# First stage in longer instructions, with places of split weights as three of 8 KB

## The chip, the cores and the metric

The kernel runs on one core of a Trainium2 chip. The metric is the device time in microseconds (us), the median of several runs. The core has five engines that matter here, each with a queue that is worked off in order: TensorE (PE in the profile, its weight loads PEld), VectorE (DVE), ScalarE (ACT), GpSimd (POOL) and SyncE (SP), which issues nearly all loads. Matmuls write to PSUM, eight banks of 2 KB per partition; everything else lies in SBUF, 128 partitions wide.

## The reference

One transformer layer on 256 tokens of width 2048, in fp32. Nine vectors ("ada") of width 2048 come from a condition c, and each of the three parts shifts and scales its input by them. FFN width is 5632.

```python
def _swiglu(h, w_in, w_out):
    gate, up = jnp.split(h @ w_in, 2, axis=-1)
    return (jax.nn.silu(gate) * up) @ w_out

def _layer(x, c, w_ada, b_ada, ffn1_w_in, ffn1_w_out, ...):
    ada = (jax.nn.silu(c) @ w_ada + b_ada)[:, None, :]
    sh1, sc1, g1, sh2, sc2, g2, sh3, sc3, g3 = jnp.split(ada, N_ADA, axis=-1)
    h = _swiglu(_modulate(x, sh1, sc1), ffn1_w_in, ffn1_w_out)
    x = _layernorm(ALPHA * x + 0.5 * (1 + g1) * h, ln1_g, ln1_b)
    h = _token_mixer(_modulate(x, sh2, sc2), w_in, ..., w_out)      # attention and mLSTM
    x = _layernorm(ALPHA * x + (1 + g2) * h, ln2_g, ln2_b)
    h = _swiglu(_modulate(x, sh3, sc3), ffn2_w_in, ffn2_w_out)
    return _layernorm(ALPHA * x + 0.5 * (1 + g3) * h, ln3_g, ln3_b)
```

`_modulate(x, shift, scale)` is `layernorm(x) * (1 + scale) + shift`.

## The kernel before

**Products.** Every large product is made of three matmuls on fp32r parts (`mm3`): a value is split into hi (rounded) and lo (the rest), and hi by hi, hi by lo and lo by hi are added up in PSUM. The activations are split once (`xhi`, `xlo`). The weights are split chunk by chunk as they come in (`load_w`): one load of 1 MB into one of three "raw" places, then per half chunk a cast on ACT (hi, line 145) and a subtraction on DVE (lo = raw - hi, line 146). Six places of 4 KB per partition hold the hi halves and six the lo halves.

**Stage one** is the first FFN's input product for the first 12 of 22 groups of 256 hidden columns, with their up halves. It begins before the ada vectors are known: the 2048 input rows are worked in four groups j of 512, since the group j needs only the quarter of shift and scale that `first_ada(j)` has computed. Per group there are 12 chunks i (even: gate columns, odd: up columns) of 512 rows by 512 columns; each is 48 matmuls 128x256, with starts 0.113 us apart, 5.4 us in all. That gives 48 chunks, here numbered 12 j + i. A chunk's result fills two banks (tiles s), and `first_in` adds it up over j in SBUF: group 0 is copied by ACT (line 738), groups 1 to 3 are added by DVE (line 740), one bank at a time. The parts lie in `hT` (places hT_0 to hT_3) and, for the last chunk of a group, in the unused half of `gate`. In group 3 the finished pair goes through Silu (ACT, line 744) into a small tile `sgs` and a product (DVE, line 745), each per 128x256.

**The ada work beside it.** While group j is multiplied, `first_ada(j+1)` loads 16 rows of 0.5 MB of w_ada (tiles ar), twelve of them by twos in raw places, four in places of their own, and DVE accumulates each into `acc` (lines 158, 160). Four column sums on PE (line 691, tiles cp and cq, one bank each) turn the accumulator into columns; DVE adds the bias (`scsh`, line 693), ACT scales the transposed input by them and splits it (lines 292, 295; xlo is DVE's line 297). In group 3, DVE accumulates for later ada vectors instead (`pump`).

**Then** `ffn_in` computes the other 10 groups of hidden columns (tiles gu_f, weights f1i), the output products follow (o_f), the mixer (fv, mv: loads of 4 x 128 rows by 512 or 520 columns through `cols_form_b`; mo, pr_f), and the second FFN (gu, f2i, f2o).

**Order.** The program is written as generators that are drawn in turn; a scheduler puts each engine's instructions into one fixed queue by their expected readiness, and loads are issued by SP in one queue, each when its place is free. PSUM is two pools for the whole kernel: five banks for results (`mm_tile`) and three for the rest (`aux_tile`); a tile takes the next bank in turn and waits for whoever last read it.

## Time and profile before

| | |
|---|---|
| runs | 1969.59, 1971.78, 1976.58 us; median 1971.78 |
| profiled execution | 1967.35 us, of which the span 1965.6 |
| mean granted TensorE clock | 0.995 |
| busy: PE, DVE, ACT | 1900.2 (97%), 1486.1 (76%), 944.3 (48%) us |
| data moved | 510.91 MB, mean 260 GB/s |
| stage one | from 37.85 to 316.2 us |

Times in the trace are us from the start of the span. A row of the timeline has start, duration, engine, line, operation, result<-inputs, shape and, in brackets, how long the engine had been idle and who released it; "x2" joins two instructions in a row. A row of a group has the count, the busy time, the mean of one in ns and the idle time ahead of it with its releasers. A row of waits has the sum, the count and the longest. Matmul ends are modelled, so what an engine loses is read from the distance of the starts.

### The profile page before, as it was taken

The page shows a single profiled execution, that of the slowest core. Times are in us where ns is not written, and L with a number is a line of the kernel's source. Part 1 is how long each engine was busy: PE and PEld are TensorE (multiplying, and loading weights), DVE is VectorE, ACT ScalarE, POOL GpSimd, SP SyncE. Part 2 cuts the span into 40 slices and gives each one's busy share as a digit, 9 for nine tenths or more (in the row PEclk, how much of TensorE's full clock was granted, in tenths as well). Part 3 has the DMA queues.
Part 4 walks back from the last instruction along what each step waited for, and adds up shares of the span by engine and source line. Part 5 has one row for each costly group of instructions (what it writes and reads, how often), then busy time and mean ns, then how long its engine had stood idle before and what let it go on. Part 6 is the DMA issues. An engine that isn't in the chain of part 4 may idle for free.

```text
span 1965.6 us, 32416 instructions
## 1 busy us (share of the span) xinstructions
PE 1900.2 (97%) x13201; PEld 1736.7 (88%) x13201; DVE 1486.1 (76%) x1827; ACT 944.3 (48%) x1328; POOL 19.6 (1%) x34
## 2 busy tenths in 40 slices
PE   3999999999999999999999999999999999999997
PEld 3999999999988888588999876899999999988886
DVE  7788888777778898678888687778756645555776
ACT  2544354443444554645755543555444444444552
POOL 0000000000000000000000000000000000000000
PEclk9999999999999999999999999999999999999998
DMA  9999878989989785589888784898757855655552
GB/s 335 333 326 315 309 234 294 310 291 303 317 297 310 269 292 199 174 302 298 268 299 287 266 276 147 293 297 296 260 194 254 278 194 187 236 191 192 193 193 86
DMA packets 301822, 510.91 MB, mean 260 GB/s; under 512 B 10819, under 2 KB 158691, under 8 KB 300649
## 3 DMA queue, kind: packets, MB, share of 16 engines
q1 hardware_dynamic: 300808, 505.70, 76.5%
q0 software_dynamic: 864, 3.15, 0.5%
q8 instruction: 103, 1.69, 0.4%
q14 instruction: 47, 0.38, 0.1%
HBM read 506.71 MB, written 2.10 MB: 259 GB/s over the span
## 4 chain that ended last, share of the span: by engine, by line
PE 77%; DMA 9%; DVE 9%; ACT 2%; issue 2%; POOL 0%; SPq 0%; DVEq 0%; ACTq 0%; POOLq 0%
PE o_f L355 8%; PE o_f L357 8%; PE o_f L356 8%; PE gu_f L355 7%; PE gu_f L357 7%; PE gu_f L356 7%; DMA ar<-in_w_ada_dram 5%; PE s L357 3%; PE s L355 3%; PE s L356 3%; DVE acc L160 2%; PE pr_f L356 2%; PE pr_f L355 2%; PE pr_f L357 2%; PE fs L355 1%
## 5 line engine op out<-in xcount | busy, mean ns | idle before, releaser
L160 DVE SCALAR_TENSOR_TENSOR acc<-ar,csil,acc 128x1024 f32<-128x1024 f32 x242 | 307.7, 1272 | 106.7 <-DMA ar<-in_w_ada_dram 105.3
L355 PE MATMUL s<-xhi_f,hi_s 128*128 128x256 f32 x768 | 213.8, 279 | 0.8 <-ACT hi_s L145 0.6
L357 PE MATMUL s<-xhi_f,lo_s 128*128 128x256 f32 x768 | 213.1, 278 | 0.6 <-DVE lo_s L146 0.5
L356 PE MATMUL s<-xlo_f,hi_s 128*128 128x256 f32 x768 | 213.4, 278 | 0.0
L357 PE MATMUL gu_f<-xhi_f,lo_f2i 128*128 128x256 f32 x768 | 212.0, 276 | 0.0
L355 PE MATMUL gu_f<-xhi_f,hi_f2i 128*128 128x256 f32 x768 | 212.0, 276 | 0.0
L356 PE MATMUL gu_f<-xlo_f,hi_f2i 128*128 128x256 f32 x768 | 212.0, 276 | 0.0
L146 DVE TENSOR_TENSOR lo_f2i<-raw_f2i,hi_f2i 128x1024 fp32r<-128x1024 f32 x96 | 116.8, 1223 | 89.5 <-ACT hi_f2i L145 89.5
L355 PE MATMUL gu_f<-xhi_f,hi_f1i 128*128 128x256 f32 x640 | 176.8, 276 | 0.2 <-DVE hT L740 0.2
L357 PE MATMUL gu_f<-xhi_f,lo_f1i 128*128 128x256 f32 x640 | 176.7, 276 | 0.0
L356 PE MATMUL gu_f<-xlo_f,hi_f1i 128*128 128x256 f32 x640 | 176.7, 276 | 0.0
L145 ACT CAST hi_f2i<-raw_f2i 128x1024 fp32r<-128x1024 f32 x96 | 100.4, 1049 | 133.7 <-PE gu_f L356 112.4
L355 PEld LDWEIGHTS s<-xhi_f,hi_s 128*128 128x128 f32 x768 | 145.1, 189 | 1.1 <-ACT hi_s L145 0.7
L357 PEld LDWEIGHTS s<-xhi_f,lo_s 128*128 128x128 f32 x768 | 144.9, 189 | 1.1 <-DVE lo_s L146 1.1
L356 PEld LDWEIGHTS s<-xlo_f,hi_s 128*128 128x128 f32 x768 | 145.2, 189 | 0.3 <-DVE xlo_f L297 0.3
L356 PEld LDWEIGHTS gu_f<-xlo_f,hi_f2i 128*128 128x128 f32 x768 | 144.1, 188 | 0.2
L355 PEld LDWEIGHTS gu_f<-xhi_f,hi_f2i 128*128 128x128 f32 x768 | 144.1, 188 | 0.2
L145 ACT CAST hi_s<-raw_s 128x1024 fp32r<-128x1024 f32 x96 | 97.3, 1050 | 97.5 <-DMA raw_s<-in_ffn_w_in_dram 56.6
L357 PEld LDWEIGHTS gu_f<-xhi_f,lo_f2i 128*128 128x128 f32 x768 | 144.1, 188 | 0.0
L146 DVE TENSOR_TENSOR lo_f2o<-raw_f2o,hi_f2o 128x1024 fp32r<-128x1024 f32 x88 | 107.7, 1224 | 44.9 <-ACT hi_f2o L145 44.8
L355 PE MATMUL o_f<-hi_f2o,hh 128*128 128x512 f32 (+1 forms) x368 | 139.4, 379 | 0.0
L357 PE MATMUL o_f<-hi_f2o,hl 128*128 128x512 f32 (+1 forms) x368 | 138.7, 377 | 0.0
(451 smaller groups left out, 5342.0 us busy)
## 6 DMA issues: line engine op xcount, KB each, us to landing
ar<-in_w_ada_dram SPq DMA_DIRECT2D x288, 512.0 KB, 5.7
raw_s<-in_ffn_w_in_dram SPq DMA_DIRECT2D x48, 1024.0 KB, 6.0
raw_f2i<-in_ffn_w_in_dram SPq DMA_DIRECT2D x48, 1024.0 KB, 5.1
raw_f1o<-in_ffn_w_out_dram SPq DMA_DIRECT2D x44, 1024.0 KB, 6.9
raw_f2o<-in_ffn_w_out_dram SPq DMA_DIRECT2D x44, 1024.0 KB, 5.1
raw_f1i<-in_ffn_w_in_dram SPq DMA_DIRECT2D x40, 1024.0 KB, 7.7
raw_mxo<-in_w_out_dram SPq DMA_DIRECT2D x16, 1024.0 KB, 6.8
raw_fh<-in_ffn_w_in_dram SPq DMA_DIRECT2D x16, 1024.0 KB, 7.5
```

The costliest lines, as they stand in the source:

```text
L145: S.copy(hi, src)
L146: V.tensor_tensor(out=lo, in0=src, in1=hi.bitcast(F32), op=ALU.subtract)
L160: V.scalar_tensor_tensor(out=acc, in0=raw, scalar=csil[:, k:k + 1], in1=acc, op0=ALU.mult, op1=ALU.add)
L355: PE.matmul(o, ah, bh, start=start, stop=False)
L356: PE.matmul(o, ah, bl, start=False, stop=False)
L357: return PE.matmul(o, al, bh, start=False, stop=stop)
```

## The change

Four things are altered.

- The places of split weights are three of 8 KB for hi and three for lo, each for a whole chunk (`part_tiles`). Outside stage one the casts and subtractions stay as they were, half a chunk each, and write into halves of a place.
- In stage one, from its second chunk on, `load_w` is called with `wide`: ACT casts the two halves, and then one subtraction makes the low part of the whole chunk (128x2048).
- A chunk's two result banks are one tile (`mm_pair`); copies, sums, Silu and products work on 128x1024, Silu in its place. The four column sums of a group lie in one such tile (cp). For stage one PSUM is divided into three pairs and two single banks (pools pm1, pa1); these are given back before `ffn_in`, and the pools of five and three are opened there.
- Where `cols_form_b` loads 520 columns, a load has 2 x 128 rows in place of 4 x 128, so there are eight of 0.53 MB per group in place of four.

```diff
     wp.tile([P, 4, 520], F32, tag="raw", bufs=3, name="raw_place")
     gap(wp, 320, "gap_hi")
-    wp.tile([P, 1024], F32R, tag="hi", bufs=6, name="hi_place")
+    wp.tile([P, 2048], F32R, tag="hi", bufs=3, name="hi_place")
...
-    wp.tile([P, 1024], F32R, tag="lo", bufs=6, name="lo_place")
+    wp.tile([P, 2048], F32R, tag="lo", bufs=3, name="lo_place")
...
-    pm = ctx.enter_context(tc.tile_pool(name="pm", bufs=5, space=PSUM))
-    pa = ctx.enter_context(tc.tile_pool(name="pa", bufs=3, space=PSUM))
+    pm = tc.alloc_tile_pool(name="pm1", bufs=3, space=PSUM)
+    pa = tc.alloc_tile_pool(name="pa1", bufs=2, space=PSUM)
...
+    def mm_pair(name):
+        return pm.tile([P, 2, 512], F32, tag="mm2", name=name)
...
+    def part_tiles(nk, w, name):
+        return [wp.tile([P, nk, w], F32R, tag=t, bufs=3, name=f"{t}_{name}") for t in ("hi", "lo")]
+
-    def load_w(src, nk, w, name, place=None):
+    def load_w(src, nk, w, name, place=None, wide=False):
         raw = wp.tile([P, nk, w], F32, tag="raw", bufs=3, name=f"raw_{name}")
         SP.dma_start(raw, src.rearrange("(k p) n -> p k n", p=P))
-        h = nk // 2 if nk * w <= 2048 else nk // 4
-        for q in range(nk // h):
...
-            hi = wp.tile([P, h, w], F32R, tag="hi", bufs=6, name=f"hi_{name}{q}")
-            lo = wp.tile([P, h, w], F32R, tag="lo", bufs=6, name=f"lo_{name}{q}")
-            split(raw[:, q * h:(q + 1) * h, :], hi, lo)
-            for kk in range(h):
-                yield q * h + kk, hi[:, kk, :], lo[:, kk, :]
...
+        hi, lo = part_tiles(nk, w, name)
+        h = nk // 2
+        for q in range(2):
+            ks = slice(q * h, (q + 1) * h)
+            if wide:
+                S.copy(hi[:, ks], raw[:, ks])
+            else:
+                split(raw[:, ks], hi[:, ks], lo[:, ks])
+                for k in range(q * h, (q + 1) * h):
+                    yield k, hi[:, k, :], lo[:, k, :]
+        if wide:
+            V.tensor_tensor(out=lo, in0=raw, in1=hi.bitcast(F32), op=ALU.subtract)
+            for k in range(nk):
+                yield k, hi[:, k, :], lo[:, k, :]
...
-        cps = aux_tile(f"cp{j}"), mm_tile(f"cq{j}")
+        cps = mm_pair(f"cp{j}")
 
         def column(q):
-            cp = cps[q % 2][:, q:q + 2]
+            cp = cps[:, q % 2, q:q + 2]
...
-        for k, hi, lo in load_w(W1[j * 512:(j + 1) * 512, c0:c0 + 512], 4, 512, f"s{j}_{i}"):
+        for k, hi, lo in load_w(W1[j * 512:(j + 1) * 512, c0:c0 + 512], 4, 512, f"s{j}_{i}", wide=i + j > 0):
             yield 4 * j + k, hi, lo
 
     def first_in(j, i, ws):
         gu, q = i % 2, i // 2
-        pss = [mm_tile(f"s{j}_{i}_{b}") for b in range(2)]
+        ps2 = mm_pair(f"s{j}_{i}")
...
-        for b, ps in enumerate(pss):
-            f0 = 2 * NS * gu + 4 * q + 2 * b
-            part = first_part(f0, f0 + 2).rearrange("p f t -> p (f t)")
-            if j == 0:
-                S.copy(part, ps)
-            else:
-                V.tensor_tensor(out=part, in0=part, in1=ps, op=ALU.add)
-            if j == 3 and gu:
-                for f in range(f0, f0 + 2):
-                    sg = sm.tile([P, T], F32, tag="sg", bufs=2, name=f"sgs{f}")
-                    S.activation(sg, hT[:, f - 2 * NS, :], AF.Silu)
-                    V.tensor_tensor(out=hT[:, f - 2 * NS, :], in0=sg, in1=first_part(f, f + 1)[:, 0, :], op=ALU.mult)
+        f0 = 2 * NS * gu + 4 * q
+        part = first_part(f0, f0 + 4).rearrange("p f t -> p (f t)")
+        ps = ps2.rearrange("p b n -> p (b n)")
+        if j == 0:
+            S.copy(part, ps)
+        else:
+            V.tensor_tensor(out=part, in0=part, in1=ps, op=ALU.add)
+        if j == 3 and gu:
+            f1 = f0 - 2 * NS
+            g = hT[:, f1:f1 + 4, :].rearrange("p f t -> p (f t)")
+            S.activation(g, g, AF.Silu)
+            V.tensor_tensor(out=g, in0=g, in1=part, op=ALU.mult)
...
     npool.release()
+    pa.release()
+    pm.release()
+    pm = ctx.enter_context(tc.tile_pool(name="pm", bufs=5, space=PSUM))
+    pa = ctx.enter_context(tc.tile_pool(name="pa", bufs=3, space=PSUM))
     ffn_in(W1, xT, hT, NS, "f1", at(R_IN))
...
-        for u in range(4):
-            for k4, hi, lo in load_w(W[u * 512:(u + 1) * 512, c0 + col:c0 + col + cb[-1]], 4, cb[-1],
+        kn = 4 if cb[-1] <= 512 else 2
+        for u in range(KD // kn):
+            for k_, hi, lo in load_w(W[u * kn * P:(u + 1) * kn * P, c0 + col:c0 + col + cb[-1]], kn, cb[-1],
                                      f"{name}{col}_{u}"):
```

The change also reorders the queues. On DVE at the start of stage one the order before was (lo_s_10 is the first half of chunk 1's low part, ar_1_k are rows of w_ada for group 1):

```order
L146 TENSOR_TENSOR lo_s_10_311<-raw_s_1_308,hi_s_10_310 128x1024
L146 TENSOR_TENSOR lo_s_11_315<-raw_s_1_308,hi_s_11_314 128x1024
L160 SCALAR_TENSOR_TENSOR acc_1_300<-ar_1_1_368,csil,acc_1_300 128x1024 x2
L160 SCALAR_TENSOR_TENSOR acc_1_300<-ar_1_4_435,csil,acc_1_300 128x1024
L146 TENSOR_TENSOR lo_s_20_378<-raw_s_2_375,hi_s_20_377 128x1024
L160 SCALAR_TENSOR_TENSOR acc_1_300<-ar_1_5_437,csil,acc_1_300 128x1024
L146 TENSOR_TENSOR lo_s_21_382<-raw_s_2_375,hi_s_21_381 128x1024
```

and is now:

```order
L363 TENSOR_TENSOR lo_s_1_305<-raw_s_1_302,hi_s_1_304 128x2048
L163 SCALAR_TENSOR_TENSOR acc_1_295<-ar_1_1_358,csil,acc_1_295 128x1024 x2
L163 SCALAR_TENSOR_TENSOR acc_1_295<-ar_1_4_420,csil,acc_1_295 128x1024
L163 SCALAR_TENSOR_TENSOR acc_1_295<-ar_1_5_422,csil,acc_1_295 128x1024
L363 TENSOR_TENSOR lo_s_2_367<-raw_s_2_364,hi_s_2_366 128x2048
```

Both accumulations that stood around the first half of chunk 2's low part now stand ahead of the whole of it. On DVE at the end of stage one the order before was (f1i are weights of `ffn_in`; s_10 and s_11 are the last two chunks of group 3, and the sum into gate is that of the very last):

```order
L740 TENSOR_TENSOR hT_3_111<-hT_3_111,s_10_0_3440 128x512
L740 TENSOR_TENSOR hT_3_111<-hT_3_111,s_10_1_3441 128x512
L146 TENSOR_TENSOR lo_f1i_0_10_3652<-raw_f1i_0_1_3649,hi_f1i_0_10_3651 128x1024
L146 TENSOR_TENSOR lo_f1i_0_11_3680<-raw_f1i_0_1_3649,hi_f1i_0_11_3679 128x1024
L160 SCALAR_TENSOR_TENSOR acc_0_3007<-ar_0_12_3707,csil,acc_0_3007 128x1024
L146 TENSOR_TENSOR lo_f1i_1_00_3713<-raw_f1i_1_0_3710,hi_f1i_1_00_3712 128x1024
L740 TENSOR_TENSOR gate<-gate,s_11_0_3508 128x512
L740 TENSOR_TENSOR gate<-gate,s_11_1_3509 128x512
```

and is now:

```order
L754 TENSOR_TENSOR hT_3_111<-hT_3_111,s_10_3157 128x1024
L149 TENSOR_TENSOR lo_f1i_0_1_3355<-raw_f1i_0_1_3352,hi_f1i_0_1_3354 128x1024 x2
L163 SCALAR_TENSOR_TENSOR acc_0_2784<-ar_0_13_3467,csil,acc_0_2784 128x1024
L163 SCALAR_TENSOR_TENSOR acc_0_2784<-ar_0_14_3526,csil,acc_0_2784 128x1024
L754 TENSOR_TENSOR gate<-gate,s_11_3220 128x1024
L149 TENSOR_TENSOR lo_f1i_1_0_3414<-raw_f1i_1_0_3411,hi_f1i_1_0_3413 128x1024
```

Rows 13 and 14 of the later ada vector stand ahead of the last sum now, where before row 12 was the last there; one low half stands behind it. On PE the first matmul of `ffn_in` is, in both, the one behind the last of s_11. Now:

```order
L368 MATMUL s_11_3220<-xhi_f_120,hi_s_11_3223 128x256
L369 MATMUL s_11_3220<-xlo_f_121,hi_s_11_3223 128x256
L370 MATMUL s_11_3220<-xhi_f_120,lo_s_11_3224 128x256
L368 MATMUL gu_f_0_3291<-xhi_f_120,hi_f1i_0_0_3295 128x256 [waits DVE_49,Activation_49]
L369 MATMUL gu_f_0_3291<-xlo_f_121,hi_f1i_0_0_3295 128x256
L370 MATMUL gu_f_0_3291<-xhi_f_120,lo_f1i_0_0_3296 128x256
```

The value of DVE's counter that this matmul waits for is reached by the sum into gate of s_11 (line 754), since its bank lies in the pair that this chunk held. Before, the same wait was for the second sum of s_9 (line 740), and the other gu_f of the pair waited for the first of s_10.

## The prediction

> **What bounds the kernel now.** I read the page's shares and slices first, then the waits and groups of stage one (38 to 317 us), then each stop of TensorE there.

> ```profile
> PE 1900.2 (97%) x13201; PEld 1736.7 (88%) x13201; DVE 1486.1 (76%) x1827; ACT 944.3 (48%) x1328; POOL 19.6 (1%) x34
> PE   3999999999999999999999999999999999999997
> PEclk9999999999999999999999999999999999999998
> ```

> TensorE is the bound in every slice but the first and the last. Faster VectorE work pays only where TensorE stops. It stops in stage one at these places, and 316.10 is the stage's last matmul:

> ```profile
> 55.28 0.51 PE L357 MATMUL s<-xhi_f,lo_s 128*128 128x256 f32 x2 [0.52 <-DVE lo_s L146]
> 104.59 0.61 PE L691 MATMUL cp<-trir,acc 128*128 128x1 f32 x4 [0.51 <-DVE scsh L693]
> 177.11 0.61 PE L691 MATMUL cp<-trir,gate 128*128 128x1 f32 x4 [2.60 <-DVE scsh L693]
> 310.95 0.38 PE L355 MATMUL s<-xhi_f,hi_s 128*128 128x256 f32 x1 [0.21 <-DVE hT L740]
> 316.10 0.28 PE L357 MATMUL s<-xhi_f,lo_s 128*128 128x256 f32 x1
> 316.21 0.28 PE L355 MATMUL gu_f<-xhi_f,hi_f1i 128*128 128x256 f32 x1
> 316.96 0.38 PE L355 MATMUL gu_f<-xhi_f,hi_f1i 128*128 128x256 f32 x1 [0.24 <-DVE hT L740]
> ```

> Starts are 0.11 us apart when nothing waits, so by starts these cost 0.68, 0.67, 2.76, 0.37 and 0.40: 4.9 us, 0.25% of the time. That is all that can be won there. A gain over 0.3% (5.9 us, about what a measurement of this kernel can tell from no change) has no place to come from; a loss has no such limit.

> **The change part by part.** *Longer VectorE instructions.* Their rows:

> ```profile
> L146 DVE TENSOR_TENSOR lo_s<-raw_s,hi_s 128x1024 fp32r<-128x1024 f32 x96 | 114.1, 1219 | 28.0 <-ACT hi_s L145 28.0
> L740 DVE TENSOR_TENSOR hT<-hT,s 128x512 f32<-128x512 f32 x66 | 42.1, 679 | 0.0
> L745 DVE TENSOR_TENSOR hT<-sgs,hT 128x256 f32<-128x256 f32 x20 | 7.5, 417 | 0.0
> 89.40 2.36 DVE L146 TENSOR_TENSOR lo_s<-raw_s,hi_s 128x1024 fp32r<-128x1024 f32 x2 [1.15 <-ACT hi_s L145]
> 91.90 0.28 PE L357 MATMUL s<-xhi_f,lo_s 128*128 128x256 f32 x1
> ```

> Two lows take 2.36, so the second starts 1.14 after the first, though one is busy for 1.22. Two sums of 128x512 take 1.27 (rows below), 0.60 apart. Per 512 elements that is 0.54, and 0.06 fixed. Joined are 47 pairs of lows, 36 of sums and 18 (24 products to 6): 101 x 0.06 = 6 us of VectorE in the stage's 279. Under a busy TensorE that is worth nothing by itself.

> [...]

> *Lows of a whole chunk* come later for their first user. Before, the first half is ready after one cast and one subtraction; now after two casts (2.00) and one subtraction of 2.36-0.06 = 2.3: about 2.06 later. The second half, and the raw place with it, is 0.9 later (4.35 from landing, before 3.45). It counts where lows are late already, behind loads in j=0:

> ```profile
> 50.59 1.05 ACT L145 CAST hi_s<-raw_s 128x1024 fp32r<-128x1024 f32 x1 [3.26 <-DMA raw_s<-in_ffn_w_in_dram]
> 52.65 1.06 ACT L145 CAST hi_s<-raw_s 128x1024 fp32r<-128x1024 f32 x1
> 53.10 0.49 PE L357 MATMUL s<-xhi_f,lo_s 128*128 128x256 f32 x2
> 54.01 1.22 DVE L146 TENSOR_TENSOR lo_s<-raw_s,hi_s 128x1024 fp32r<-128x1024 f32 x1
> ACT hi_s L145 <- DMA raw_s<-in_ffn_w_in_dram: 56.6, 20, 7.2
> ```

> Chunk 2 (its casts start at 50.59): both casts in a row end at 52.6, the low at 54.9, or 56.2 if the accumulation that now stands ahead of it is late; I take 55.2. The first use stood at 53.10: 2.1 lost, less the 0.68 of 55.28 that goes: **+1.5** (0 to +2.5). Chunk 1 stops about 1.1, inside these 2.1. Chunk 9's first low was done at 90.63 for a use at 91.90, 1.3 to spare where 2.06 is needed; TensorE, later by 1.5, then has 0.7 left. But the three raw places serve 12 chunks and 6 pairs of ada rows a group, so a place turns in two chunks, and each turn is up to 0.9 longer, in j=0 up to the tenth chunk four turns, 3.6. I take **+1.3** (0 to +4.4). After that casts wait more for TensorE than for loads, and lows have over 4 us to spare.

> *Column sums.* At 104.59 the accumulator's column sum waited for its bank; the order now has other work there: **-0.7**. At 177 the wait is an ada load's:

> ```profile
> 174.50 1.28 DVE L160 SCALAR_TENSOR_TENSOR acc<-ar,csil,acc 128x1024 f32<-128x1024 f32 x1 [3.40 <-DMA ar<-in_w_ada_dram]
> 176.90 0.15 DVE L693 TENSOR_TENSOR scsh<-cp,bcol 128x2 f32<-128x2 f32 x1
> ```

> TensorE comes 2.1 later (1.5+1.3-0.7). A load that lands at a fixed time gives that back; one that waits for a place doesn't. Half: -1.1. One tile now holds all four column sums, so each waits for the addition of the last (0.15 and a turn between engines), and the last quarter's xlo stands behind a sum of 1.2: +0.5, and +0.2 at the next group. **-0.4** (-2.8 to +3).

> *The end of the stage.* Stage one now has its own pools: three pairs of banks and two. They are given back before ffn_in, whose first gu_f takes the first bank, in the pair of the very last sum (gate, chunk s_11 of j=3). So that matmul waits for VectorE's last sum; before, it waited for the sum of s_9, two chunks earlier. VectorE's rows there:

> ```profile
> 260.27 1.22 DVE L146 TENSOR_TENSOR lo_s<-raw_s,hi_s 128x1024 fp32r<-128x1024 f32 x1 [1.88 <-ACT hi_s L145]
> L160 DVE SCALAR_TENSOR_TENSOR acc<-ar,csil,acc 128x1024 f32<-128x1024 f32 x12 | 15.4, 1279 | 3.6 <-DMA ar<-in_w_ada_dram 3.6
> 316.23 1.27 DVE L740 TENSOR_TENSOR hT<-hT,s 128x512 f32<-128x512 f32 x2
> 317.42 2.35 DVE L146 TENSOR_TENSOR lo_f1i<-raw_f1i,hi_f1i 128x1024 fp32r<-128x1024 f32 x2
> 319.69 1.27 DVE L160 SCALAR_TENSOR_TENSOR acc<-ar,csil,acc 128x1024 f32<-128x1024 f32 x1
> 322.03 1.27 DVE L740 TENSOR_TENSOR gate<-gate,s 128x512 f32<-128x512 f32 x2
> ```

> Its last sum ended at 323.30, 7 us after TensorE's last matmul, and nobody cared. From 260.27, where it was level with TensorE (it waited for a cast), that is 63.0, of which 3.8 were waits (3.6 for ada loads). Now: 59.2 of work, less 34 joints x 0.06 = 2.0, less one low half that moved behind the sum (1.14), plus two accumulations that moved ahead of it (2.4): 58.5. It ends at 318.8 without a wait, at 322.5 with 3.7 as before. TensorE would be there at 315.8 (316.21 without the 0.37 of 310.95, which three pairs remove): a stop of 3.0 or 6.7; less the 0.77 of before: +2.3 or +5.9. I take **+5.9**, as the ada loads stand in the same traffic. If VectorE were level at the last chunk, two lows, two accumulations and a sum (5.9) against a chunk's 5.4 leave 0.5, a last sum 1.2 and a handover 0.1: +1.0, the low end. One more late load of 3.4 (the longest here, at 174.50): +9.3, the high end.

> *The clock behind it.* Such a stop can cost a stretch at half clock:

> ```profile
> 843.97 0.39 PE L355 MATMUL b_fv<-hi_fv,xhi_mx 128*128 128x264 f32 x1 [1.95 <-ACT og L1144]
> 842.00:845.40 3.40, 1.45 (x10) 1.27 (x10) 2.69 (x3) 3.39 (x10) 0.00 (x0) 0.99 0.71 238
> 845.40:848.80 3.40, 3.40 (x18) 3.40 (x17) 2.00 (x6) 1.69 (x4) 0.00 (x0) 0.50 0.81 258
> 174.50:181.00 6.50, 3.90 (x35) 3.89 (x35) 6.50 (x13) 4.56 (x10) 0.73 (x1) 1.00 0.51 165
> ```

> After 1.95 us idle 3.4 us ran at 0.50, so 1.7 were lost; after 2.60 idle (177.11) the clock stayed at 1.00. A stop of 6.7 is far longer than both: **+1.7** (0, or 3.4 with one at chunk 2). [...]

> *The rest.* Places of 8 KB are returned a chunk at a time, loads of 520 columns are halved:

> ```profile
> ACT hi_f2i L145 <- PE gu_f L356: 112.4, 70, 2.2
> raw_fv<-in_w_in_dram SPq DMA_DIRECT2D x4, 1040.0 KB, 8.5
> ```

> The casts wait for TensorE there, so they run some two chunks (10.9 us) ahead of it; a place that comes back half a chunk (2.7) later is covered by that. Without that cover it would be 2.7 once per stage. The halved loads bring 0.53 MB in a place that held 1.06, so the three places hold half as much; TensorE needs 2.7 for each, 8.2 a turn, against a landing of 4.9 to 8.5 and a split of 2: 0, up to +4. Together **0** (-2 to +4).

> Sum: 1.5+1.3-0.7-0.4+5.9+1.7 = **+9.3**. The profiled execution of 1967.35 (span 1965.6) becomes 1976.7; it lies 4.4 below the median of the runs, 1971.78, so the median becomes 1981.

> **The rivals.** *VectorE keeps level (not slower).* If it reaches the last chunk level with TensorE, the end costs 1.0 and no half clock; with chunk 2 at 0, -0.7 at 104 and -2.6 at 177 that is -2.3: 1969.5. Deciding is whether its last sum can start when TensorE ends. For it: lighter VectorE, earlier ada loads. Against: it was 7 us late, 3.8 by waits that the change doesn't touch. [...] *No waits for loads at the end:* +2.3, no half clock: sum +4.0, 1975.8, within 0.3%. *The ring decides:* in j=0 and 1 each turn loses 0.9, 12 turns, 10.8 in place of 1.3: 1990.5; for it the 56.6 us of casts waiting for loads, against it the spare time after j=0. *The first gu_f doesn't wait for the last sum:* 1973.5; the order shows that wait.

> **How the numbers follow.** The forecast (+6 to +15) 0.60; ring 0.10; end without waits 0.15; no wait 0.05; VectorE level 0.10. Slower 0.70; of the other 0.30 same takes 0.24, and 0.06 is for faster. Own range of the forecast 1978 to 1987; for 8 in 10, 1971 to 1990.

> **What would show it.** Right: a stop of 4 to 8 us before the first gu_f (line 368), released by VectorE's sum into gate (754), a clock near 0.5 after it, a stop of about 2 at a low of line 363 before 60 us, none at 104. Wrong: gu_f starting within 2 us of the last s matmul, or stops of the ring, casts waiting for raw_s, all through j=1.

## The result, and the profile after

The changed kernel takes 2000.72 us (median of 4 runs, 1997.74 to 2009.48) against 1970.68 (4 runs, 1960.81 to 1976.58) beside it: a ratio of 1.0167 with a 95% interval of 1.0143 to 1.0191. It is 30 us slower; 9.3 were forecast, and 1978 to 1987 as the range. The profiled execution took 2000.38, of which the span is 1998.5, 32.9 more than before.

The page of the changed kernel: shares of the engines, then the slices of TensorE and of its clock.

```profile
PE 1910.4 (96%) x13201; PEld 1745.3 (87%) x13201; DVE 1468.3 (73%) x1726; ACT 922.7 (46%) x1298; POOL 19.6 (1%) x34
PE   3999997999999999999999999999999999999997
PEclk9998998999999999999999999999999999999999
```

VectorE has 101 instructions less and is busy for 17.8 us less. TensorE has the same 13201 matmuls, is busy for 10 us more, and two new dents show in the slices of 50 us: the clock below 9 tenths in the fourth (150 to 200 us), clock and share in the seventh (300 to 350). Both lie in stage one, which now ends at 340.08 where it ended at 316.21. TensorE's stops there, in its timeline (start, duration, engine, line, operation; in brackets the idle time and who ended it):

```profile
55.86 0.38 PE L370 MATMUL s<-xhi_f,lo_s 128*128 128x256 f32 x1 [1.79 <-DVE lo_s L363]
110.53 0.61 PE L704 MATMUL cp<-trir,acc 128*128 128x1 f32 x4 [2.12 <-DVE scsh L706]
184.40 0.77 PE L704 MATMUL cp<-trir,gate 128*128 128x1 f32 x4 [3.50 <-DVE scsh L706]
328.77 0.28 PE L370 MATMUL s<-xhi_f,lo_s 128*128 128x256 f32 x1
340.08 0.55 PE L368 MATMUL gu_f<-xhi_f,hi_f1i 128*128 128x256 f32 x1 [11.04 <-DVE gate L754]
```

By the distance of starts, of which 0.11 is there without a stop, these are 2.07, 2.40, 3.78 and 11.31 us. Behind three of them the clock is halved. Windows of the same trace (from:to, length, then busy time and count of PE, PEld, DVE, ACT, POOL, the granted clock, the DMA share and GB/s):

```profile
113.00:116.40 3.40, 3.40 (x18) 3.40 (x17) 3.40 (x7) 3.06 (x5) 0.00 (x0) 0.50 1.02 383
184.70:194.90 10.20, 10.20 (x49) 10.20 (x49) 5.28 (x9) 3.53 (x8) 0.73 (x1) 0.50 0.59 167
329.00:340.10 11.10, 0.06 (x2) 0.05 (x1) 7.39 (x8) 2.94 (x3) 0.00 (x0) 0.61 0.90 281
340.10:345.00 4.90, 4.90 (x23) 4.90 (x24) 4.44 (x4) 0.42 (x1) 0.54 (x1) 0.50 0.56 187
```

In the second one TensorE works without a gap for 10.2 us at half speed: 5.1 us lost to a stop of 3.8. Comparing the start of the same matmul in both traces (after less before) gives a balance of the whole span. Of the 23.6 us between forecast and measurement, 4.0 and 6.1 lie at the two groups of column sums, 4.8 at the first gu_f and 7.1 behind the stage:

| place | forecast, us | measured, us |
|---|---|---|
| start of the stage | 0 | +0.5 |
| chunks 1 and 2 | +1.5 | +1.7 |
| rest of j=0 (stops at 89 and 95 us) | +1.3 | +1.6 |
| column sums at 110 (before: 104) | -0.7 | +3.3 |
| column sums at 184 (before: 177) | -0.4 | +5.7 |
| chunks 24 to 47 | 0 | +0.4 |
| stop at the first gu_f | +5.9 | +10.7 |
| half clock behind it | +1.7 | +1.9 |
| everything behind stage one | 0 | +7.1 |
| sum | +9.3 | +32.9 |

**The column sums.** Why they stop is read from VectorE's queue, which is worked off in order. Its timeline in the changed kernel, around the first and the second group of column sums:

```profile
106.25 0.75 DVE L161 TENSOR_SCALAR gate<-ar,csil 128x1024 f32<-128x1024 f32 x1 [4.44 <-DMA ar<-in_w_ada_dram]
106.92 2.28 DVE L363 TENSOR_TENSOR lo_s<-raw_s,hi_s 128x2048 fp32r<-128x2048 f32 x1
109.12 1.28 DVE L163 SCALAR_TENSOR_TENSOR gate<-ar,csil,gate 128x1024 f32<-128x1024 f32 x1
110.32 0.16 DVE L706 TENSOR_TENSOR scsh<-cp,bcol 128x2 f32<-128x2 f32 x1
...
181.86 1.28 DVE L163 SCALAR_TENSOR_TENSOR acc<-ar,csil,acc 128x1024 f32<-128x1024 f32 x1 [3.31 <-DMA ar<-in_w_ada_dram]
183.06 1.22 DVE L754 TENSOR_TENSOR hT<-hT,s 128x1024 f32<-128x1024 f32 x1
184.19 0.16 DVE L706 TENSOR_TENSOR scsh<-cp,bcol 128x2 f32<-128x2 f32 x1
```

The second column sum writes into the tile that the first one's addition (L706) still reads. That addition takes 0.16 us, but it stands behind a low part of 2.28 and an accumulation of 1.28, and both stand behind an accumulation that waited 4.44 us for a row of w_ada. The matmul at 110.53 starts 0.21 after the addition began. In the second group the same happens behind a wait of 3.31.

**Why the rows of w_ada are late.** The waits for loads between 38 and 108 us, before:

```profile
ACT hi_s L145 <- DMA raw_s<-in_ffn_w_in_dram: 6.9, 5, 3.3
DVE acc L160 <- DMA ar<-in_w_ada_dram: 0.6, 1, 0.6
```

and in the changed kernel:

```profile
ACT hi_s L357 <- DMA raw_s<-in_ffn_w_in_dram: 15.3, 8, 3.7
DVE gate L161 <- DMA ar<-in_w_ada_dram: 4.4, 1, 4.4
DVE acc L163 <- DMA ar<-in_w_ada_dram: 3.6, 4, 1.4
```

Casts waited 15.3 us in place of 6.9, accumulations 8.0 in place of 0.6. Rows of w_ada and weights share three raw places and one queue of loads, so it is near at hand that places given back later, by the whole lows, hold up everything issued behind them. That isn't shown. These waits move without any change: in the same window the kernel before once more (e10_same, below) has

```profile
ACT hi_s L145 <- DMA raw_s<-in_ffn_w_in_dram: 10.7, 6, 3.1
DVE acc L160 <- DMA ar<-in_w_ada_dram: 3.1, 2, 2.4
```

and whole lows without the pairs of banks (e2_wide, below) have no more than that:

```profile
ACT hi_s L354 <- DMA raw_s<-in_ffn_w_in_dram: 11.2, 5, 3.4
DVE acc L160 <- DMA ar<-in_w_ada_dram: 2.9, 4, 1.0
```

What made the loads of the change late stays open.

**The end of the stage.** VectorE's last instructions before the first gu_f, in the timeline of the changed kernel, and what its accumulations waited for between 282 and 345 us (us, times):

```profile
329.13 1.22 DVE L754 TENSOR_TENSOR hT<-hT,s 128x1024 f32<-128x1024 f32 x1
330.26 2.36 DVE L149 TENSOR_TENSOR lo_f1i<-raw_f1i,hi_f1i 128x1024 fp32r<-128x1024 f32 x2
332.53 1.28 DVE L163 SCALAR_TENSOR_TENSOR acc<-ar,csil,acc 128x1024 f32<-128x1024 f32 x1
337.52 1.28 DVE L163 SCALAR_TENSOR_TENSOR acc<-ar,csil,acc 128x1024 f32<-128x1024 f32 x1 [3.71 <-DMA ar<-in_w_ada_dram]
338.73 1.21 DVE L754 TENSOR_TENSOR gate<-gate,s 128x1024 f32<-128x1024 f32 x1
```

```profile
  DMA ar<-in_w_ada_dram: 7.0, 5
```

The queue is the one that was forecast: one sum, two lows, two accumulations, the last sum. The waits for w_ada on the way there, from 282 us on, add up to 7.0 us where 3.7 had been put in, and the last sum ends at 339.94.

### The profile page after: what moved, and what is told of

It is laid out like the page before. It is cut to its first block, busy times and chain, and to the rows that moved or that the text cites. A ratio compares the mean times of both kernels' runs of the same rounds, so it can differ in the third digit from the quotient of the medians.

```text
span 1998.5 us, 31957 instructions
## 1 busy us (share of the span) xinstructions
PE 1910.4 (96%) x13201; PEld 1745.3 (87%) x13201; DVE 1468.3 (73%) x1726; ACT 922.7 (46%) x1298; POOL 19.6 (1%) x34
## 3 DMA queue, kind: packets, MB, share of 16 engines
q8 instruction: 103, 1.69, 0.3%
## 4 chain that ended last, share of the span: by engine, by line
PE 66%; DMA 14%; DVE 13%; issue 3%; ACT 3%; POOL 0%; ACTq 0%; DVEq 0%; SPq 0%; POOLq 0%
DMA ar<-in_w_ada_dram 11%; PE o_f L368 8%; PE o_f L370 8%; PE o_f L369 8%; PE gu_f L368 7%; PE gu_f L370 7%; PE gu_f L369 7%; DVE acc L163 3%; PE s L369 2%; PE s L370 2%; PE s L368 2%; DVE lo_s L363 1%; PE fs L370 1%; PE fs L368 1%; PE fs L369 1%
## 5 line engine op out<-in xcount | busy, mean ns | idle before, releaser
L148 ACT CAST hh<-hT 128x512 fp32r<-128x512 f32 x128 | 78.7, 622 | 191.7 <-PE o_f L369 191.7
L357 ACT CAST hi_s<-raw_s 128x1024 fp32r<-128x1024 f32 x94 | 94.4, 1047 | 116.4 <-DMA raw_s<-in_ffn_w_in_dram 59.9
L149 DVE TENSOR_TENSOR hl<-hT,hh 128x512 fp32r<-128x512 f32 x128 | 86.5, 690 | 77.8 <-ACT hh L148 77.8
```

What stands on the lines that cost most here:

```text
L148: S.copy(hi, src)
L149: V.tensor_tensor(out=lo, in0=src, in1=hi.bitcast(F32), op=ALU.subtract)
L357: S.copy(hi[:, ks], raw[:, ks])
```

## The experiments

Each ratio is against the kernel before, run beside it on the same chip, with its 95% interval. "Stage one" is the time from the first s matmul to the first gu_f in the profile: 278.4 us before, 301.7 with the change. Single profiles of one and the same program differ by 6 us behind that stage (below), so only stage one is compared between profiles, and all else by medians. A difference of medians between two experiments is one between separate series, each beside its own runs of the kernel before.

**Places alone** (e4_places): the kernel before with three places of 8 KB and with the halved loads of 520 columns; lows, sums and PSUM stay.

```diff
-    wp.tile([P, 1024], F32R, tag="hi", bufs=6, name="hi_place")
+    wp.tile([P, 2048], F32R, tag="hi", bufs=3, name="hi_place")
...
-        h = nk // 2 if nk * w <= 2048 else nk // 4
...
+        kn = 4 if cb[-1] <= 512 else 2
```

> The kernel before with two things of the change alone: places of split weights as three of 8 KB, and halved loads of 520 columns; stage one as before. Theory A (the loss behind stage one, 6.6 us in the profile of the change, comes from these two): about +6 us against before, 1977, with the later waits of the change (a longer one at o_f near 541 us, others at pr_m and nps near 955) in its profile and stage one unchanged. Theory B (that loss comes from VectorE's queue after the new stage one, not from the places): within 2 us of before, 1971.

1977.34 us against 1968.61, 1.0048 (1.0020 to 1.0075). Stage one takes 279.3: at most 1 of the 23 us comes from the places. But some 8 us come from outside the stage, where the forecast had 0.

**Places and whole lows** (e2_wide): e4_places with low parts of 128x2048, PSUM and sums as before.

```diff
-        for k, hi, lo in load_w(W1[...], 4, 512, f"s{j}_{i}"):
+        for k, hi, lo in load_w(W1[...], 4, 512, f"s{j}_{i}", wide=i + j > 0):
```

> As the run with the places alone, and with the lows of whole chunks (128x2048) in stage one; sums per bank, pools of five and three banks as before. Theory A: wide lows cost 3.3 us up to the tenth chunk (1.7 at chunk 2, 1.6 at chunks 8 and 9) and nothing at the end of the stage: 3 to 4 us above the run with the places alone, no stop over 1 us at the first gu_f. Theory C (the wide lows make every ada load later and so the stops at the column sums too): stops of over 2 us at the column sums near 108 and 180 us with half clock behind them, 10 us above the run with the places alone.

1986.47 us, 1.0090 (1.0065 to 1.0115). Stage one takes 288.5, 9.2 more than with the places alone, as theory C had it. Its stops of TensorE:

```profile
55.44 0.51 PE L367 MATMUL s<-xhi_f,lo_s 128*128 128x256 f32 x2 [1.86 <-DVE lo_s L360]
98.31 0.39 PE L365 MATMUL s<-xhi_f,hi_s 128*128 128x256 f32 x1 [2.22 <-ACT hi_s L354]
185.02 0.61 PE L701 MATMUL cp<-trir,gate 128*128 128x1 f32 x4 [3.35 <-DVE scsh L703]
```

The whole lows alone bring the stop at chunk 2, a second one at 98 where a cast had waited for its load, and a longer one at the second group of column sums (2.60 idle before). At the first group, where theory C expected one, there is none.

**The change with narrow lows** (e3_narrow).

```diff
-        ... wide=i + j > 0):
+        ... wide=False):
```

> The changed kernel with lows of half chunks (128x1024) again; pairs of banks, joint sums, new pools and places kept. Theory A: chunks 2, 8 and 9 lose nothing (-3.3 us), the stops at the column sums stay, the stop before the first gu_f stays at 8 to 12 us: 1996 against 2000.7 for the change. Theory C (wide lows make the column sums late): the stops near 110 and 184 us and their half clock go too, 9 us more: 1987.

1987.69 us, 1.0093 (1.0068 to 1.0118). Stage one takes 288.2: 13.5 of its 23 us go with the whole lows. What is left, by starts 1.8 and 8.1 us:

```profile
176.12 0.60 PE L704 MATMUL cp<-trir,gate 128*128 128x1 f32 x4 [1.50 <-DVE scsh L706]
326.72 0.55 PE L368 MATMUL gu_f<-xhi_f,hi_f1i 128*128 128x256 f32 x1 [7.86 <-DVE gate L754]
```

With e2_wide: the stop at 110 appears where the joint tile and the whole lows come together; the stop at the first gu_f needs only the pairs and their pools.

**Pools given back later** (e6_later): ffn_in uses the pairs too, and the pools are exchanged after it.

```diff
+            pair = mm_pair(f"gu_{tag}{j}") if tag == "f1" else None
...
+    ffn_in(W1, xT, hT, NS, "f1", at(R_IN))
     pa.release()
     pm.release()
     pm = ctx.enter_context(tc.tile_pool(name="pm", bufs=5, space=PSUM))
     pa = ctx.enter_context(tc.tile_pool(name="pa", bufs=3, space=PSUM))
-    ffn_in(W1, xT, hT, NS, "f1", at(R_IN))
```

> The changed kernel, but stage one's pools are kept through ffn_in, whose gu_f take pairs of banks, and are given back after it. VectorE's order up to the last sum is the same. Theory A (the first gu_f waits for the last sum because the pools are given back there): the stop of 11 us and the half clock behind it (2 us) go, the first gu_f starts within 1 us of the last matmul of stage one, at most 2 us come back where the pools are given back later: -11 to -13 us against the change, 1988 to 1990. Theory D (VectorE is late anyway and the stop moves on to the next thing that TensorE needs of it, the lows of ffn_in): under -5 us, 1996 or more.

2000.82 us, 1.0161 (1.0132 to 1.0190): the gain of theory A doesn't come. The time is theory D's, but not by its way: the stop before the first gu_f is gone, and one as long stands, not at a low of ffn_in, but where the pools are now exchanged, before the first output product:

```profile
567.32 0.77 PE L368 MATMUL o_f<-hi_f1o,h 128*128 128x512 f32 x1 [10.95 <-DVE hT L394]
```

The stop goes where the pools are given back: the first user of the new pools waits for the last readers of the old ones (11.04 us idle in the change, 10.95 here), and in both places those are VectorE's latest work.

**The last sum's banks freed by a copy** (e7_copy): ACT copies the result of the last chunk out of PSUM, VectorE adds the copy.

```diff
+            if j == 3 and i == NS - 1:
+                out_ = scp.tile([P, 4 * T], F32, name=f"sout{i}")
+                S.copy(out_, ps)
+                ps = out_
             V.tensor_tensor(out=part, in0=part, in1=ps, op=ALU.add)
```

> The changed kernel, but ACT copies the very last chunk's result out of PSUM, and VectorE adds it later from SBUF; so the pools can be given back without VectorE's last sum. VectorE's order ahead of that sum is the same. Theory A (the stop is VectorE's lateness, made a stop by the pools' return): first gu_f within 2.5 us of the last matmul of stage one (VectorE's sum of the chunk before ended 1.4 us behind TensorE in the profile of the change), no half clock behind it, and as ffn_in's own pools leave VectorE time, no stop elsewhere: -10 to -12 us against the change, 1989. Theory D (VectorE's lateness has to be paid somewhere): the stop comes back at lows of ffn_in or at o_f, under -4 us, 1997 or more.

1995.88 us, 1.0147 (1.0110 to 1.0183). The stop falls from 11.3 to 3.1 by starts, but the copy stands in ACT's queue behind a Silu that waits for VectorE's sum of the chunk before (timelines of TensorE, then of ACT):

```profile
333.36 0.58 PE L368 MATMUL gu_f<-xhi_f,hi_f1i 128*128 128x256 f32 x1 [2.81 <-ACT sout L756]
...
330.40 1.06 ACT L762 ACTIVATE hT<-hT 128x1024 f32<-128x1024 f32 x1 [3.33 <-DVE hT L758]
331.37 1.03 ACT L148 CAST hi_f1i<-raw_f1i 128x1024 fp32r<-128x1024 f32 x1
332.30 1.00 ACT L756 COPY sout<-s 128x1024 f32<-128x1024 f32 x1
```

Of the gain of 8 us at this place 6.7 are left over the whole of stage one (295.0 against 301.7), as the stop at the second column sums is longer in the same trace (5.5 us, and 13.65 us of half clock around it). The median is 5 us below the change, between the 1989 and the 1997 of the two theories.

**The halved loads alone** (e8_loads): the kernel before with nothing but the eight loads of 0.53 MB in place of four of 1.06.

```diff
+        kn = 4 if cb[-1] <= 512 else 2
-        for u in range(4):
+        for u in range(KD // kn):
```

> The kernel before with the halved loads of 520 columns alone (eight of 0.53 MB in place of four of 1.06 MB), places of 4 KB as before. With the places it was +7 us in the profile (+8.7 in the medians). Theory E (the places of 8 KB cost, since a place comes back a whole chunk at a time): no loss, 0 to -3 us (the stop of 1.95 us at b_fv with its half clock went in the run with the places and the loads). Theory F (the smaller loads cost): +3 to +7 us between 843 and 1090 us.

1975.91 us (12 runs) against 1968.01 (23 runs), 1.0033 (1.0017 to 1.0050). Within the intervals this is the loss of e4_places: about 6 us that lie outside stage one (279.2 us). Where in the mixer they go, its trace doesn't show beyond the spread of single profiles.

**Whole lows from the second group on** (e9_wide1): e2_wide, but narrow in j=0.

```diff
-        ... wide=i + j > 0):
+        ... wide=j > 0):
```

> As the run with wide lows on the old pools, but lows are wide from the second group of rows (j = 1) on. Theory A (wide lows cost where loads are late, that is in j = 0, by the raw places' longer turn, and the stop at 185 us follows from ada loads that this made late): as the run with the places alone, 1977 to 1979, stop at the column sums near 177 us at 2.8 us as before. Theory G (the stop at the column sums comes from wide lows of j = 1 standing in VectorE's queue): the stop near 180 us stays at 3.6 us with half clock, 1981 to 1983.

1974.53 us (10 runs), 1.0033 (1.0012 to 1.0054): no more than the halved loads, so whole lows in the three later groups cost nothing. Stage one takes 276.4, 2.0 less than before. The column sum that stood at 185.02 in e2_wide comes 11.9 us earlier and without a stop:

```profile
173.09 0.53 PE L701 MATMUL cp<-trir,gate 128*128 128x1 f32 x4
```

Nothing was edited there, and j=1 still has its whole lows. So the long stop in j=1 comes from those of j=0, by the lateness they leave or by the order that goes with it (the sum stands 0.13 of a chunk earlier in TensorE's queue here); that whole lows in j=1 itself cause it is refuted. That there is no stop at all is partly luck of one profile: e12_whole (below) has the same stage one, takes 279.1 for it, and there the sum stops for 1.6 us by starts with 6.83 us of half clock behind it.

**Another bank for the first gu_f** (e1_banks): the new pools are opened in the other order, so the first gu_f lies in a bank whose last use was earlier.

```diff
-    pm = ctx.enter_context(tc.tile_pool(name="pm", bufs=5, space=PSUM))
     pa = ctx.enter_context(tc.tile_pool(name="pa", bufs=3, space=PSUM))
+    pm = ctx.enter_context(tc.tile_pool(name="pm", bufs=5, space=PSUM))
+    for b in range(2):
+        mm_tile(f"skip{b}")
```

> The changed kernel with the new pools opened in the other order, so that the first two gu_f lie in a bank of the chunk before the last and in one that stage one's results never used. Theory H (the wait is for the bank: the first gu_f takes the pair of the last chunk, as the prediction had it): the stop before the first gu_f falls from 11 to under 3 us. Theory I (a new pool waits for the whole of the old one): the stop stays at 8 to 12 us.

One run, 1996.8 us. The stop stays, behind the same sum, with 8.15 us by starts:

```profile
336.58 0.55 PE L368 MATMUL gu_f<-xhi_f,hi_f1i 128*128 128x256 f32 x1 [7.87 <-DVE gate L754]
```

So it is not the bank that decides: the wait is for the whole pool of pairs.

**The kernel before once more** (e10_same), as a program of its own.

> The kernel before once more, with nothing changed in what it does: how far two series of one program lie apart. Theory K (a series differs from another by chance alone): ratio 1.000 within 0.2%, and the stop at o_f near 541 us, 2.2 us before, anywhere between 1 and 5 us. Otherwise the 6.5 us measured for the halved loads alone are in doubt.

1971.30 us (12 runs) against 1969.53 (23), 1.0011 (0.9995 to 1.0027). Single runs of one program reach from 1961.71 to 1978.83. Its profiled span is 1972.1 where the first profile of before had 1965.6, and the difference lies behind stage one (278.6 against 278.4 in it). The +7.1 of the balance above is therefore no clean reading of the change: the profile that the forecast started from was a short one.

**Two repairs** (e11_repair): the change with narrow lows in j=0 (as in e9_wide1) and the copy of e7_copy.

> The changed kernel with both repairs: lows of half chunks in the first group of rows (wide from the second on), and the very last chunk's result copied out of PSUM by ACT. Theory A (the loss adds up from three parts: wide lows in j = 0 about 10, the stop at the pools' return 8 to 13, places and loads 7): only the last remains, 1975 to 1980, stops at the column sums near 105 and 177 us under 3 us, first gu_f within 3 us. Theory L (joint sums and the one tile of column sums cost by themselves): 1985 or more, with stops of over 3 us at the column sums.

1987.49 us, 1.0093 (1.0071 to 1.0115), 8.4 less than e7_copy and outside the 1975 to 1980 of theory A; the time is theory L's. By starts 2.9 and 4.2 us were left at the two places, each followed by half clock:

```profile
176.14 0.80 PE L704 MATMUL cp<-trir,gate 128*128 128x1 f32 x3 [2.64 <-DVE scsh L706]
323.59 0.58 PE L368 MATMUL gu_f<-xhi_f,hi_f1i 128*128 128x256 f32 x1 [3.95 <-ACT sout L756]
```

**Whole loads again** (e12_whole): e9_wide1 with the loads of 520 columns whole, each split into two places.

```diff
+        if nk * w > 2048:
+            for q in range(2):
+                hi, lo = part_tiles(nk // 2, w, f"{name}{q}")
+                for kk in range(nk // 2):
+                    k = q * nk // 2 + kk
+                    split(raw[:, k, :], hi[:, kk], lo[:, kk])
+                    yield k, hi[:, kk, :], lo[:, kk, :]
+            return
```

> As the run with wide lows from the second group on (places of 8 KB, old pools), but the loads of 520 columns are whole again (four of 1.06 MB, each split into two places). Theory F (the halved loads cost all that is left): 1968, no difference from before within 0.2%, perhaps 1 or 2 us less since stage one lost 2.5 us in its profile. Theory E (the coarse places cost it): 1974 to 1977.

1968.74 us (12 runs), 0.9996 (0.9979 to 1.0013). With the loads whole nothing is left of the loss: the places of 8 KB and the whole lows behind j=0 cost nothing, and bring nothing either.

**Whole lows in column halves** (e13_cols): e2_wide, with the low parts of j=0 in two instructions, both behind both casts, each for the columns that are used first or second.

```diff
+            if wide == "cols":
+                r4, h4, l4 = (x.rearrange("p k (b h n) -> p k b h n", b=2, h=2) for x in (raw, hi.bitcast(F32), lo))
+                for c in range(2):
+                    V.tensor_tensor(out=l4[:, :, :, c], in0=r4[:, :, :, c], in1=h4[:, :, :, c], op=ALU.subtract)
```

> As the run with wide lows on the old pools (1986.5), but in the first group of rows each chunk's low is made in two halves by columns, both behind the second cast: the first use has its half 1.1 us earlier than with one wide low, the raw place comes back as late as with it. Theory A (the raw places' longer turn costs): as with wide lows, 1984 to 1988. Theory J (what costs is that the first use waits for the whole low): half of the 12 us between that run and the one with narrow lows in the first group goes, 1979 to 1982.

1982.68 us, 1.0077 (1.0051 to 1.0103): 3.8 us less than e2_wide, between the ranges of the two theories. The intervals overlap, and stage one is no shorter in the profile (288.8 against 288.5), so whether an earlier first use returns anything over the whole stage is not shown. Inside the stage TensorE began the last chunk of j=0 3.4 us later than before, where e2_wide was 6.3 and e9_wide1 0.2 later; but the stop of j=1 came all the same, and longer:

```profile
184.88 0.59 PE L706 MATMUL cp<-trir,gate 128*128 128x1 f32 x2 [5.93 <-DVE scsh L708]
```

**The change with whole loads** (e14_whole): the edit of e12_whole on the changed kernel.

> The changed kernel with the loads of 520 columns whole again. Theory F (they cost about 6 us whatever stage one does): 6 us less than the change, 1994 to 1996, stage one unchanged (first gu_f 20 to 25 us later than before). Theory M (what the loads cost is hidden once VectorE and TensorE are shifted against each other): as the change, 1999 to 2002.

1998.30 us (5 runs, 1988.52 to 1999.37), 1.0143 (1.0106 to 1.0181). That is 2.4 us less than the change by medians; -6 lies inside the intervals, and so does 0. This run doesn't tell them apart.

**Two repairs and whole loads** (e15_both): the same edit on e11_repair.

> The run with both repairs (narrow lows in the first group, the last chunk copied out by ACT), with the loads whole as well. Theory F: 5 to 7 us less than that run, 1981 to 1983; what is left stands before the first gu_f (9 us later than before, a stop of 4 us behind ACT's copy with half clock behind it).

1981.20 us (10 runs), 1.0054 (1.0033 to 1.0075): 6.3 less than e11_repair. The halved loads cost the same 6 us here as in e8_loads and in e12_whole.

**Three pools** (e16_three): the change with narrow lows in j=0 and whole loads, and with each pair of banks in a pool of its own. They are given back separately, and the first gu_f lies in the pair of the chunk before the last.

```diff
-    pm = tc.alloc_tile_pool(name="pm1", bufs=3, space=PSUM)
+    pms = [tc.alloc_tile_pool(name=f"pm1{b}", bufs=1, space=PSUM) for b in range(3)]
...
-        return pm.tile([P, 2, 512], F32, tag="mm2", name=name)
+        pairs[0] += 1
+        return pms[(pairs[0] - 1) % 3].tile([P, 2, 512], F32, tag="mm2", name=name)
...
-    pm.release()
+    for p_ in reversed(pms):
+        p_.release()
```

> The changed kernel with narrow lows in the first group and whole loads, and with stage one's three pairs of banks as three pools instead of one, so that the new pools of ffn_in lie over the pools of the chunks before the last alone: the first gu_f waits for VectorE's sum of the chunk before the last, all else in VectorE's order alike. Theory A (a pool that is given back whole makes VectorE's lateness a stop; nothing else in the joint sums costs): stop before the first gu_f under 3 us in place of 8 to 11, first gu_f 1 to 5 us later than before, 1970 to 1975. Theory L (joint sums and the one tile of column sums cost by themselves): 1979 or more.

1974.63 us (12 runs), 1.0025 (1.0006 to 1.0044), within the 1970 to 1975 of theory A. Stage one takes 280.7. TensorE's last matmul of the stage and the first gu_f, then VectorE beside them:

```profile
318.70 0.28 PE L380 MATMUL s<-xhi_f,lo_s 128*128 128x256 f32 x1
319.12 0.36 PE L378 MATMUL gu_f<-xhi_f,hi_f1i 128*128 128x256 f32 x1
...
317.76 1.22 DVE L764 TENSOR_TENSOR hT<-hT,s 128x1024 f32<-128x1024 f32 x1
325.08 1.28 DVE L165 SCALAR_TENSOR_TENSOR acc<-ar,csil,acc 128x1024 f32<-128x1024 f32 x1 [2.64 <-DMA ar<-in_w_ada_dram]
326.29 1.21 DVE L764 TENSOR_TENSOR gate<-gate,s 128x1024 f32<-128x1024 f32 x1
```

The first gu_f starts 0.14 us after the sum of s_10 has ended. The very last sum ends 8.4 us later, its accumulation having waited for w_ada as before, and TensorE runs on. The joint sums, Silu and products and the whole lows behind j=0 are all still there, so it was not their length that cost the time, but whom they made wait. Narrow lows in j=0 and whole loads do not take the stop away by themselves: e15_both has both, with the three pairs in one pool, and still stops for 3.4 us by starts at the first gu_f. Some 5 us over the kernel before are left (1.0025); about 2 of them lie in stage one, and where the others lie is not known.

No version is measurably faster than the kernel before; e12_whole equals it.

**The sum of it.** From differences of medians, and behind "or" from differences of the ratios: halved loads 6 to 8 us (e8_loads 0.33%; from e12_whole to e9_wide1 5.8 or 7.3; from e15_both to e11_repair 6.3 or 7.7); whole lows in j=0 8 to 12 (from e11_repair to e7_copy 8.4 or 10.6; from e9_wide1 to e2_wide 11.9 or 11.2); pairs and the return of their pools 9 to 15 (from e4_places to e3_narrow 10.4 or 8.9; from e2_wide to the change 14.3 or 15.2). Together 23 to 35, around the 30 measured. The parts need not simply add up: the stop at 110 belongs to two of them together.

## Why the prediction was right and wrong

**Right.** That the kernel becomes slower, since longer instructions off the bound can win nothing and stops of TensorE can lose; chunk 2 (+1.5 forecast, +1.7, with the stop of about 2 us at its low); the rest of j=0 (+1.3, +1.6); that the first gu_f stops, behind VectorE's last sum, with the clock near 0.5 after it (+1.7, +1.9); that the places alone cost nothing (e12_whole).

**Column sums at 104: the step that failed first.** "The order now has other work there: -0.7" took the stop to be gone. It was +3.3 (1.6 of longer stop, 1.7 of half clock behind it), because the step looked at the bank of before and not at the joint tile: the second column sum now waits for the addition of the first. The text had seen that wait at 177 and priced it as "0.15 and a turn between engines". The instruction does take 0.16 us. What counts is its place in a queue worked off in order: behind a load that was 4.44 us late, a low of 2.28 and an accumulation of 1.28. e3_narrow (joint tile, no whole lows) and e2_wide (whole lows, no joint tile) both have no stop at this place, so it takes the two together; e15_both, with the joint tile and narrow lows in j=0, has one of 1.0 us by starts there. Why the load was that late is open, as said above: the forecast priced the longer turn of the places by what TensorE loses in j=0 and had no term for what VectorE then brings along, and no run shows that the turn made the load late.

**Column sums at 177: wrong sign** (-0.4 forecast, +5.7 measured). "A load that lands at a fixed time gives that back" was weighed half and half with "one that waits for a place doesn't". The load did come later with the rest, so nothing was given back: VectorE waited 3.31 for it in place of 3.40, 7.4 us later. The stop grew by only 0.9; 4.8 are half clock, 10.2 us of it, where the forecast allowed 1.7 for any one stop. From e2_wide to e9_wide1 only the lows of j=0 change, and the long stop goes with them (in e12_whole, with the same stage one, 1.6 us by starts are left), by the lateness they leave or by the order. They are not all of it: e11_repair, with narrow lows in j=0 and the joint tile, still has 2.64 us idle there and 6.83 us of half clock.

**The end: right mechanism, size off** (+5.9, +10.7; the upper bound was +9.3). The term "VectorE's waits for ada loads" was taken as 3.7, as before, and measured 7.0, the longest 3.71 directly ahead of the last sum. That is 3.3 of the 4.8 missing; the other 1.5 is not traced to a term. The way there was also told wrongly. "The first bank, in the pair of the very last sum" made it a matter of the bank; e1_banks keeps the stop with another bank, e6_later moves it with the return of the pools, e16_three removes it by returning the pairs one by one.

**The rest: not 0.** The halved loads were put at "0, up to +4", by a comparison of the three places' turn (8.2) with landing and split (4.9 to 8.5, and 2). They cost 6 to 8 us in three independent pairs of kernels; the fourth, e14_whole, doesn't tell. Whether this is the turn of the places is not shown; no run told apart the number of loads from the amount that waits in a place. The +7.1 in the profile holds this loss and the short profile of before (e10_same, +6.5 with nothing changed); how it divides is not shown.

**The rivals.** The ring was named with 10.8 and a chance of 0.10, as casts that wait for loads all through j=1. They wait hardly more than before: over stage one these waits rose from 56.6 to 59.9 us only, and in j=1 they fell from 29.1 (108 to 178 us) to 25.1 (112 to 190). The forecast's reading that casts wait more for TensorE than for loads once j=0 is over was wrong, though: before the change they waited 49.7 us for loads and 32.3 for TensorE between 108 and 315 us. The loss of the rest of j=0 was as small as forecast; what was lost behind it stands at stops that VectorE ends. VectorE keeping level, no waits for loads at the end, and a first gu_f that doesn't wait are refuted by the stop of 11.31.

**Longer instructions.** The whole lows, as a group (busy in ns, smallest/median/largest):

```profile
L363 DVE TENSOR_TENSOR lo_s<-raw_s,hi_s x47: 2283/2290/2295, 45.7 to 320.0; 128x2048 fp32r<-128x2048 f32 x47
```

The next instruction starts 2.20 us after one of them (106.92 to 109.12), where two narrow ones take 2 x 1.14: 0.08 saved; a sum of 128x1024 is followed after 1.13 (329.13 to 330.26), where two narrow ones took about 1.20: 0.07. The forecast of 0.06 a joint holds.

**The clock.** The stop of 2.40 at 110.53 had a half clock behind it (0.50 from 113.0 to 116.4), and TensorE was busy without a gap through 10.2 us at 0.50 from 184.7. The rows of the forecast (1.95 us idle, then 0.50) held, yet one stretch a stop was too little: behind the stop of 184.40 stood three. The rival without waits for loads put no half clock behind a stop of 3.0. The runs showed both: none behind 2.76 by starts at 177.11 before, 6.83 us of it behind 2.9 by starts in e11_repair.

## What to carry to other kernels

Price a new wait by the place of the awaited instruction in its engine's queue, not by its duration: read what stands ahead of it, and take every load in that queue as late as the latest one that the trace shows. Look for the last reader of all the buffers that a pool gives back together: here the next user stood idle for 11.04 us behind it, for 7.87 with another bank (e1_banks), and with the pairs given back one by one its stop went (e16_three). So return them one by one, or where the readers are ahead. A short stop of TensorE is not harmless because it is short: behind the 2.40 us at 110.53 stood 3.4 us at half clock (1.7 lost), behind the 3.78 at 184.40 10.2 us (5.1 lost).

## What the runs showed of the hardware

What goes ahead of one is read best by counting how long TensorE streams columns in a window of this grid: the distance of starts that a product needs when nothing waits, 0.113 us for 256 columns (counted double for products in plain fp32, whose starts at line 630 of the change lie 0.43 apart for 512 columns, against 0.23 at its line 368), and nothing for the column sums, which have one column. The count was made afterwards, on these traces, for the windows at full clock between 45 and 1930 us. All 59 windows with more than 2.2 us without streaming were followed by one at 0.50, 12 of 37 with 2.0 to 2.2, and 3 of 9171 with less. So in these traces a stop counted by how it fell on the grid and by what was multiplied beside it. The 2.60 idle at 177 us before left 2.0 and 1.8 us in its two windows and stayed without consequence. The 2.12 at 110.53 in the change left 1.8 and, with the column sums behind it, 2.5, and the half clock came.

How long the half clock lasts under full load varied from one window to three (184.7 in the change), and nothing in the traces tells which it will be.

One program, run 12 to 23 times, spreads over 14 to 18 us, and two profiles of it differed by 6.5 us of span, though they were equal to 0.4 us up to the first gu_f. Effects of a third of a per cent were to be had from many runs only.
